# Layer 0 of a two-layer trunk: token halves joined at levels 32 and 64, and two recurrence chains stepped in one tick

## The chip, the cores and the metric

The kernel runs on one core of a Trainium2 chip. The metric is device microseconds (us) of one execution, as the median of several runs. Before the change the median of 3 runs was 2139.13 us (2138.96 to 2139.31). TensorE is called PE below, its weight loads PEld, VectorE DVE, ScalarE ACT, GpSimd POOL and SyncE SP.

## The reference

A decoder trunk of two layers over 256 tokens with 2048 features, all in float32. Layer 0 is the recurrent one, and the change lies in its mixer:

```
proj = h @ w_in                                   # 2048 -> 6144 columns
x_lru, y_lru, q_h, f_h, v_h, g_h = split(proj)    # 1024 columns each
lru  = rg_lru(conv(x_lru)) * gelu(y_lru)          # 4 heads, gated linear recurrence
hg   = hgrn2(q_h, f_h, v_h, g_h)                  # 8 heads of 128
mix  = concat([lru, hg]) @ w_out

# hgrn2, per head (lb is a learned lower bound)
q = silu(q_raw);  f = lb + (1 - lb) * sigmoid(f_raw);  k = (1 - lb) * sigmoid(-f_raw)
o[t] = sum over s <= t of (q[t] * prod(f[s+1..t]) . k[s]) v[s]
o    = rms_norm(o) * g_norm * silu(g_raw)
```

The reference runs hgrn2 in chunks of 64 tokens; written out over all tokens it is the sum above. After the mixer follow a residual add, a squared-ReLU MLP, and layer 1 with dilated attention and another MLP. Those parts aren't touched.

## The kernel before

**Products.** Every float32 operand is split into a high and a low float32r part, and a product is three matmuls: high times high, high times low, low times high. A *unit* is a weight block of 1 MB. SP loads it into a `raw` tile (L148), ACT casts it to `hi` (L130), DVE subtracts to get `lo` (L131). There are three tiles each of `raw`, `hi` and `lo`, and a unit is fetched three ahead, so the cast of a new unit waits until PE has released the tile of the unit that just ended.

**The input projection of layer 0** runs in *steps* of 512 output columns, in the order `ORDER` (L1150): v0 x0 x1 G0 q0 f0 q1 f1 G1 v1 g0 y0 g1 y1. The letter names the group, the digit its half. A step (`tokens_group`, `tokens`) takes four units of 24 matmuls each, 12 for either token half, and ends with two evictions (L371) into a `tk` tile. G0 and G1 aren't projections: they are the recurrence gates (`lru_gates`), 48 matmuls of 256 columns in four blocks of 12 that go in turn to a `p` bank and a `pl` bank.

**Ticks.** The rest of the mixer is interleaved by hand with the projection. After every 12 projection matmuls comes a *tick*: two to a unit, eight to a step. The table `TICKS` (L1151) says which lanes advance at each tick; a lane is a list of generators, and one advance runs to the next `yield`. PE executes in exactly the order that is written (`mm` and `turn` chain every matmul to the one before); the order on the other engines is made by the scheduler from priorities, and is fixed once the program is built. The lanes:

- **a** and **b**: `hgrn`, one generator for each pair of heads; lane a has chains 0 and 2, lane b chains 1 and 3. A chain has 12 steps: q (transpose, sigmoid), f (transpose, sigmoids), the diagonal (four matmuls of 128 columns into bank `pd` or `pt`), eight levels c = 1, 2, 4, ... 128, and the output (matmuls with v into `pd` or `pt`, squares, copy).
- **c**: `lru_in` four times (three steps each: transposes into bank `po` and a first convolution, a second convolution, a split into `bufb` by L269 and L270), then `lru_gelu` and `lru_out`.
- **e**: `lru_scan`, with Tanh, Exp and square roots on ACT and the scan on DVE.
- **d**: `finish`, two steps for each pair of heads: first the norm and the gate, on DVE, with a sigmoid; then four transposes into `po` and the split into `bufb` by L272 (ACT) and L273 (DVE).

**A level** of `hgrn` joins blocks of c tokens to blocks of 2c. For every pair of neighbouring blocks it needs the scores between keys of the first and queries of the second block. Up to level 64 it computes, for each of two heads and each token half of 128, one fp32 matmul: stationary all 128 keys of the half, moving the 64 queries that stand in second blocks (`halves(..., True)`), into a bank of `pl` (two buffers, shared by both chains and by G0 and G1). The wanted blocks are picked from it: up to level 16 by a masked copy on DVE (L532), at 32 and 64 by copies on ACT (L538, L540). Then a multiplication on DVE (L547) brings queries and keys to the next level, in place, and the products of decays (L550) go to a small scratch. Level 128 has one matmul of 128 columns per head (L523) and a copy (L524). The chain's data lie in `xall`: a slot of 2048 columns for a chain holds the queries and keys (1024), the decays f (512, last read at level 1) and the scratch.

`po`, `pd` and `pt` are one PSUM bank each, so a new use waits until the engines have read the last one. The weights that are waited for, the evictions and the chains' work share ACT and DVE in one queue each.

## Time and profile before

| what | value |
|---|---|
| median of 3 runs | 2139.13 us |
| the profiled execution | 2137.32 us |
| its span, first to last instruction | 2135.5 us |
| mean granted clock of PE | 0.998 |
| ACT busy | 1308.2 us, 61% |
| DMA | 500.12 MB, mean 234 GB/s |

The profile is of one execution. Timeline rows have the start in us from the span's start, the length, engine, line, operation, tiles and shapes; in brackets the idle time of the engine before it, and what ended that. `xN` merges N records that follow each other. A line can be that of a helper: L223 is every matmul, L226 every transpose, so the tile names tell the parts apart. An fp32 matmul leaves two records, a float32r matmul one. The ends of matmuls are modelled and overlap the next start, so what PE needs for something is read from start to next start. In rows of windows, the columns are the stretch and its length, the busy time and the count of PE, PEld, DVE, ACT and POOL, then the granted clock, the share of the DMA engines and GB/s.

In this execution the steps q0 to y1 lie at about 79 to 332 us of the span; G0 begins at 73.4 and G1 at 182.5.

### The profile page before, as it was taken

The numbers are of one execution on the slowest core, as the hardware profiler recorded it, in microseconds if no ns is written. First come the engines' busy times: TensorE is split into PE (matmuls) and PEld (weight loads), VectorE is DVE, ScalarE is ACT, GpSimd is POOL, SyncE is SP. The second block draws the span as 40 slices with busy tenths as digits, with TensorE's granted clock in tenths as the row PEclk, the third lists the DMA queues.
The fourth block names the chain that finished last, engine by engine and source line by source line (L and its number), as shares of the span: only waits on it lengthen the run. The fifth ranks groups of instructions, "written<-read, shape, count | busy, mean of one in ns | idle before, by whom it ended". The sixth has DMA issues, their size and how long they took to land.

```text
span 2135.5 us, 24906 instructions
## 1 busy us (share of the span) xinstructions
PE 2119.7 (99%) x9854; PEld 1766.3 (83%) x9854; DVE 1780.0 (83%) x1687; ACT 1308.2 (61%) x1307; POOL 72.3 (3%) x89
## 2 busy tenths in 40 slices
PE   9999999999999999999999999999999999999998
PEld 7888878888888888888888888888888888888887
DVE  7665758988888888889998888798988987988897
ACT  7646546666466566557665666566755755755664
POOL 0000000000000000000000000000000000000000
PEclk9999999999999999999999999999999999999999
DMA  8444446678878787887788667667878778787885
GB/s 342 179 166 150 157 179 205 212 244 266 250 243 258 255 253 234 278 248 242 223 285 247 215 217 213 220 206 238 246 236 280 240 249 263 249 250 241 273 261 157
DMA packets 70164, 500.12 MB, mean 234 GB/s; under 512 B 7840, under 2 KB 8096, under 8 KB 10272
## 3 DMA queue, kind: packets, MB, share of 16 engines
q1 hardware_dynamic: 57888, 412.99, 51.0%
q0 software_dynamic: 11872, 84.94, 21.3%
q8 instruction: 77, 1.26, 0.2%
q10 hardware_dynamic: 288, 0.61, 0.1%
q14 instruction: 39, 0.32, 0.0%
HBM read 496.41 MB, written 2.10 MB: 233 GB/s over the span
## 4 chain that ended last, share of the span: by engine, by line
PE 99%; DVE 1%; ACT 0%; DMA 0%; issue 0%
PE p L223 62%; PE pd L223 15%; PE po L223 14%; PE pt L223 3%; PE pl L226 2%; PE pl L223 2%; DVE lo L131 0%; ACT hi L130 0%; PE po L226 0%; DMA both_in<-in_head 0%; DVE xc L604 0%; PE pd L226 0%; PE pt L226 0%; ACT xall L1137 0%; ACT z L302 0%
## 5 line engine op out<-in xcount | busy, mean ns | idle before, releaser
L130 ACT CAST hi<-raw 128x2048 fp32r<-128x2048 f32 (+1 forms) x364 | 659.3, 1817 | 536.0 <-PE p L223 334.8
L131 DVE TENSOR_TENSOR lo<-raw,hi 128x2048 fp32r<-128x2048 f32 (+1 forms) x364 | 788.9, 2171 | 219.8 <-ACT hi L130 218.6
L223 PE MATMUL p<-hi,bufa 128*128 128x512 f32 x2000 | 650.4, 394 | 1.0 <-ACT bufa L272 1.0
L223 PEld LDWEIGHTS p<-hi,bufa 128*128 128x128 f32 x2000 | 376.1, 188 | 78.2 <-ACT bufa L272 1.2
L223 PE MATMUL p<-hi,bufb 128*128 128x512 f32 x1264 | 404.9, 390 | 0.0
L223 PE MATMUL p<-lo,bufa 128*128 128x512 f32 x1000 | 389.8, 390 | 0.0
L131 DVE TENSOR_TENSOR lo<-s,hi 128x2048 fp32r<-128x2048 f32 x120 | 274.2, 2285 | 12.0 <-ACT hi L130 9.7
L223 PEld LDWEIGHTS p<-hi,bufb 128*128 128x128 f32 x1264 | 237.3, 188 | 49.0
L130 ACT CAST hi<-s 128x2048 fp32r<-128x2048 f32 x120 | 229.6, 1913 | 50.4 <-PE po L223 22.5
L223 PE MATMUL p<-lo,bufb 128*128 128x512 f32 x632 | 245.9, 389 | 0.0
L223 PEld LDWEIGHTS p<-lo,bufa 128*128 128x128 f32 x1000 | 188.3, 188 | 37.5 <-DVE lo L131 0.4
L223 PEld LDWEIGHTS p<-lo,bufb 128*128 128x128 f32 x632 | 118.7, 188 | 24.2
L223 PE MATMUL pd<-hi,bufa 128*128 128x512 f32 x352 | 116.6, 393 | 0.0
L223 PE MATMUL p<-hi,formx 128*128 128x512 f32 x352 | 116.3, 391 | 0.0
L131 DVE TENSOR_TENSOR lo<-t,hi 128x2048 fp32r<-128x2048 f32 x40 | 91.5, 2288 | 15.7 <-ACT hi L130 15.7
L223 PE MATMUL po<-hi,bufb 128*128 128x512 f32 (+1 forms) x320 | 102.3, 386 | 0.0
L223 PE MATMUL p<-hi,formh 128*128 128x512 f32 x288 | 94.5, 389 | 0.0
L159 DVE TENSOR_TENSOR s<-s,raw 128x2048 f32<-128x2048 f32 x40 | 91.3, 2282 | 1.4 <-DMA raw<-in_w_qkv 1.4
L159 DVE TENSOR_TENSOR s<-raw,t 128x2048 f32<-128x2048 f32 x40 | 91.4, 2284 | 0.2 <-DMA raw<-in_w_o 0.2
L223 PE MATMUL po<-hi,bufa 128*128 128x512 f32 x256 | 84.8, 392 | 0.0
L130 ACT CAST hi<-t 128x2048 fp32r<-128x2048 f32 x40 | 76.5, 1914 | 11.6 <-PE pd L223 5.9
L223 PE MATMUL pd<-hi,bufb 128*128 128x512 f32 x256 | 83.0, 389 | 0.0
(317 smaller groups left out, 2783.0 us busy)
## 6 DMA issues: line engine op xcount, KB each, us to landing
raw<-in_w SPq DMA_DIRECT2D x224, 1024.0 KB, 6.6
raw<-in_w_in SPq DMA_DIRECT2D x45, 1024.0 KB, 4.8
raw<-in_w_qkv SPq DMA_DIRECT2D x42, 1024.0 KB, 6.6
t<-in_w SPq DMA_DIRECT2D x32, 1024.0 KB, 6.6
t<-in_w POOLq DMA_DIRECT2D x32, 1024.0 KB, 8.7
s<-in_w POOLq DMA_DIRECT2D x32, 1024.0 KB, 8.9
raw<-in_w_out SPq DMA_DIRECT2D x15, 1024.0 KB, 4.8
raw<-in_w_o SPq DMA_DIRECT2D x15, 1024.0 KB, 4.8
```

What stands on the lines that cost most here:

```text
L130: casts[:] = [after(A.copy(h, w), [])]
L131: i = V.tensor_tensor(l, w, h.bitcast(F32), OP.subtract)
L159: return V.tensor_tensor(held[to], held[x], held[y], OP.add)
L223: chain[:] = [after(T.matmul(*args, **kw), chain)]
L226: chain[:] = [after(T.transpose(out_, in_, ident), chain)]
```

## The change

Three things are altered, all in layer 0.

- At levels 32 and 64 the keys of first blocks are copied by ACT from both token halves into one contiguous tile `kc` of 128 columns per head (in the room of f), at the end of the level before. One matmul per head then takes `kc` as stationary and the 128 queries of second blocks of both halves as moving operand: two matmuls of 128 columns instead of four of 64. The diagonal blocks of the result are copied to the scores one by one: four copies at level 32 and two at level 64, where there were two and one.
- Lanes a and b advance in the same tick, every second tick, instead of in turn.
- The other lanes are placed around that. In x1 and f0 a tick is left free before the fourth step of lane c. Lane d begins in y0 and has its first four steps done by the end of g1. In y1 the ticks of c and d are apart, and those of o0 (the first step of the output projection) are one later.

```
             plf = pl.rearrange("p h j c -> p h (j c)")
...
-            for h in range(2):
-                for j in range(2):
-                    js = slice(j * P, j * P + P)
-                    mm(pl[:, h, j], kq[:, h, js], halves(qp[:, h, js], c, True), start=True, stop=True)
+            if c >= 32:
+                for h in range(2):
+                    mm(plf[:, h], kc[:, h], halves(qp[:, h], c, True), start=True, stop=True)
+            else:
+                for h in range(2):
+                    for j in range(2):
+                        js = slice(j * P, j * P + P)
+                        mm(pl[:, h, j], kq[:, h, js], halves(qp[:, h, js], c, True), start=True, stop=True)
...
-            elif c == 32:
-                for n in range(2):
-                    ps_ = slice(64 * n, 64 * n + 32)
-                    A.copy(st[ps_, :, :2, 64 * n + 32:64 * n + 64], pl[ps_, :, :, 32 * n:32 * n + 32])
             else:
-                A.copy(st[:64, :, :2, 64:], pl[:64])
+                for n in range(P // c):
+                    j, at_ = divmod(2 * n * c, P)
+                    ns = slice(n * c, n * c + c)
+                    A.copy(st[at_:at_ + c, :, j, at_ + c:at_ + 2 * c], plf[ns, :, ns])
...
             c *= 2
+            if c in (32, 64):
+                at_ = slot + 1024 + 256 * (c == 64)
+                kc = xall[:, at_:at_ + 256].rearrange("p (h s) -> p h s", h=2)
+                A.copy(kc.rearrange("p h (n c) -> p h n c", c=c),
+                       kq.rearrange("p h (n two c) -> p h n two c", two=2, c=c)[:, :, :, 0])
...
 TICKS = {
-    "x1": "c c c c c c . .",
+    "x1": "c c c . c c c .",
     "q0": ". e . e . e . e",
-    "f0": "c c c c c ac b .",
-    "q1": "a b a b a b a b",
-    "f1": "a b a b a b a b",
-    "v1": "a be a be a be a be",
-    "g0": "a b a b a b a b",
-    "y0": "a b a b a b a b",
-    "g1": "a b a b a b d d",
-    "y1": "dc dc d d dc dc . .",
-    "o0": ". . c c . . . .",
+    "f0": "c c c . c c abc .",
+    "q1": ". ab . ab . ab . ab",
+    "f1": ". ab . ab . ab . ab",
+    "v1": "e ab e ab e ab e ab",
+    "g0": ". ab . ab . ab . ab",
+    "y0": ". ab . ab . ab d ab",
+    "g1": ". ab d ab d ab . d",
+    "y1": "d c d d c d c c",
+    "o0": ". . . c c . . .",
 }
```

In the changed program the lines behind the edit stand eight lower (three to eight within `hgrn`): the score copies are L543, the level's multiplication is L550, the copy to `kc` is L559. L130, L131, L223, L226, L269 to L273 and L371 keep their numbers.

More of the change, by code (lines that the diff above doesn't have):

```diff
@@ L519, in hgrn @@
             pl = psc.tile([P, 2, 2, 64], F32, name="pl", bufs=2)
+            plf = pl.rearrange("p h j c -> p h (j c)")
             if c == 128:
-                plf = pl.rearrange("p h j c -> p h (j c)")
                 for h in range(2):
```

## Prediction

> **What bounds the kernel now.** I read the page first. Part 1 gives each engine's busy share, part 4 the chain of work that ended last.

> ```profile
> PE 2119.7 (99%) x9854; PEld 1766.3 (83%) x9854; DVE 1780.0 (83%) x1687; ACT 1308.2 (61%) x1307; POOL 72.3 (3%) x89
> PE 99%; DVE 1%; ACT 0%; DMA 0%; issue 0%
> ```

> TensorE (PE) is the bound over the whole span. A change gains only what it takes off PE's own instructions or off PE's waits, and any new PE wait is paid in full. The waits of PE come next: who waited for whom, total, times, longest.

> ```profile
> PE po L226 <- DVE bufb L273: 4.8, 1, 4.8
> ...
> PE po L226 <- DVE xc L604: 0.8, 2, 0.4
> ```

> One wait of 4.8 us and two of 0.4 lie in the changed stretch (53 to 345 us). The timeline around the long one, with the granted clock from windows (third quantity from the end):

> ```profile
> 301.27 0.60 PE L226 MATMUL po<-tab__183,ho 128*128 128x128 f32 x4
> ...
> 302.17 0.63 PE L223 MATMUL p<-hi,bufa 128*128 128x512 f32 x2
> ...
> 306.26 0.62 PE L223 MATMUL p<-hi,bufa 128*128 128x512 f32 x2
> ...
> 306.94 0.39 PE L223 MATMUL p<-hi,bufa 128*128 128x512 f32 x1
> 312.13 1.09 PE L226 MATMUL po<-tab__183,ho 128*128 128x128 f32 x4 [4.80 <-DVE bufb L273]
> ...
> 319.39 0.60 PE L226 MATMUL po<-tab__183,ho 128*128 128x128 f32 x4
> ```

> ```profile
> 307.37 1.90 ACT L130 CAST hi<-raw 128x2048 fp32r<-128x2048 f32 x1 [1.91 <-PE p L223]
> ...
> 309.30 2.29 DVE L131 TENSOR_TENSOR lo<-raw,hi 128x2048 fp32r<-128x2048 f32 x1 [0.30 <-ACT hi L130]
> 311.51 0.48 DVE L273 SCALAR_TENSOR_TENSOR bufb<-po,c__91,bufb 128x256 fp32r<-128x256 f32 x1
> ```

> ```profile
> 306.90:311.50 4.60, 0.43 (x2) 0.01 (x1) 4.30 (x8) 2.88 (x4) 0.00 (x0) 1.00 0.64 228
> 311.50:315.00 3.50, 2.87 (x9) 2.51 (x10) 2.89 (x10) 0.95 (x2) 0.00 (x0) 0.51 0.63 213
> ```

> Eighteen projection matmuls start between 302.17 and 306.26, so one costs 0.227 us. The next should have started at 307.17 but started at 312.13: 4.96 us lost. The reason is a queue. The weight cast (L130) waits until PE releases a weight tile at the end of a unit, its subtraction (L131) follows, and only then DVE frees the bank `po` (L273) that PE wants. Afterwards the clock is 0.51: from 312.13 to 319.39 are 7.26 us, against 307.17 - 301.27 = 5.90 for the same work before the wait. The slow clock cost another 1.36.

> **The change, part by part.** (a) *Two matmuls for four.* Levels 32 and 64 of four chains are 8 places. The four 64-column matmuls of a level are 8 records (fp32 leaves two each); the two 128-column ones would be 4, as level 128 has now.

> ```profile
> 178.02 1.00 PE L223 MATMUL pl<-xall 128*128 128x64 f32 x8
> 178.83 0.48 PE L223 MATMUL p<-hi,bufa 128*128 128x512 f32 x1
> ...
> 181.68 1.00 PE L223 MATMUL pl<-xall 128*128 128x64 f32 x8
> ```

> ```profile
> 198.39 0.60 PE L223 MATMUL pl<-xall 128*128 128x128 f32 x4
> 198.75 0.48 PE L223 MATMUL p<-hi,bufa 128*128 128x512 f32 x1
> ...
> 201.57 0.60 PE L223 MATMUL pl<-xall 128*128 128x128 f32 x4
> ```

> From start to next start: 0.81 and 0.36. A record costs about 0.11 whether 64 or 128 columns stream. Gain 8 x 0.45 = 3.6 us. The moving side is strided and level 128's is contiguous; the 64-column ones were strided too and show no surcharge, so I take none.

> [...]

> (b) *Steps side by side.* In the order of the built program, PE leaves the projection and comes back 24 times less. After a 64-column step, twelve projection matmuls take 181.68 - 178.83 = 2.85, after a 128-column step 201.57 - 198.75 = 2.82, against 12 x 0.227 = 2.73; with the records at 0.111 each, a return costs between 0.01 (0.36 + 2.82 - 2.73 - 4 x 0.111) and 0.04 (0.81 + 2.85 - 2.73 - 8 x 0.111). I take 0.03: gain 0.7, bounds 0.2 and 1.0.

> (c) *One tick more before the fourth `lru_in` step* in x1 and f0. The two waits of 0.4 end 2.7 us before the transposes now come. A modelled end lies 0.39 - 0.227 = 0.16 behind the next possible start, so each is worth 0.57: gain 1.1.

> (d) *Norms.* All four steps of group 0 come before y1, but the wait only moves. In the built order, `finish(1,0)`'s transposes want `po`, whose last reader is again an L273 behind an L130 and an L131 that wait for the end of a unit of y1: the same chain, with y1's tick 3 instead of tick 2, so twelve more projection matmuls (2.73) cover it. Left: 4.96 - 2.73 = 2.2. Gain 2.7.

> (e) *Clock.* A wait of 2.2 is under half of the one that dropped it. The nearest row on the other side is at the start, with a granted clock of 1.00 on both sides of it:

> ```profile
> 5.88 0.50 PE L223 MATMUL p<-hi,bufa 128*128 128x512 f32 x1 [0.97 <-ACT bufa L272]
> ```

> 0.97 kept the clock, 4.80 lost it. I take no drop (gain 1.4) and keep 1.4 per wait of over 2 us as the other end.

> (f) *New wait at G0.* The third `lru_in` step of x0's second half moves from tick 6 of x1 to tick 7. In the built order its split (L269, L270) now stands behind the last eviction of x1 (L371), one more cast and one more subtraction. Rows of before there:

> ```profile
> 70.08 2.29 DVE L131 TENSOR_TENSOR lo<-raw,hi 128x2048 fp32r<-128x2048 f32 x1 [0.80 <-ACT hi L130]
> ...
> 72.29 0.69 DVE L270 TENSOR_TENSOR bufb<-xc,bufb 128x512 fp32r<-128x512 f32 x1
> 73.38 0.40 PE L223 MATMUL p<-bufb,hi 128*128 128x256 f32 x2
> ...
> 74.81 0.40 PE L223 MATMUL pl<-bufb,hi 128*128 128x256 f32 x2
> ```

> ```profile
> 73.58 0.69 ACT L371 ACTIVATE tk<-p,nr 128x512 f32<-128x512 f32 x1 [2.03 <-PE p L223]
> 74.16 1.89 ACT L130 CAST hi<-raw 128x2048 fp32r<-128x2048 f32 x1
> ```

> With G0's start as zero (73.38): eviction at 0.20, cast at 0.78, done 2.67; subtraction 2.70; L270 starts 72.29 - 70.08 = 2.21 later, 4.91, done 5.60. PE needs it for G0's third block, two blocks of 74.81 - 73.38 = 1.43 in, second matmul: 2.98. Wait 2.6. Before, the split was done by 72.98, hidden.

> (g) *New wait at G1.* Both level-32 steps now sit at the end of f1 and fill both `pl` banks; G1's second block needs the first bank. ACT's order: eviction, cast, then eight copies (L543).

> ```profile
> 181.88 0.69 ACT L371 ACTIVATE tk<-p,nr 128x512 f32<-128x512 f32 x1 [2.30 <-PE p L223]
> 182.46 1.89 ACT L130 CAST hi<-raw 128x2048 fp32r<-128x2048 f32 x1
> ...
> 184.25 0.52 ACT L538 COPY st<-pl 32x128 f32<-32x128 f32 x2
> ```

> The copies begin 184.25 - 181.68 = 2.57 after the step's start. One of half the size is not in the trace: at most L538's 0.26, at least half of it; I take 0.21, four are done at 3.4. PE wants the bank at 2 x 0.45 + 1.43 = 2.3. Wait 1.1, bounds 0.8 and 1.4.

> (h) *New wait at level 128.* Its `pl` banks are freed by level 64's four copies, which ACT's order puts behind 2 casts, 2 sigmoids, 8 Tanh and Exp, 2 table loads and 3 square roots.

> ```profile
> 190.26 0.83 ACT L254 ACTIVATE bufb<-pl,c__91 128x256 f32<-128x256 f32 x2
> 190.98 1.30 ACT L254 ACTIVATE bufb<-bufb,sp 128x256 f32<-128x256 f32 x3
> 192.30 1.28 ACT L254 ACT_TABLE_LOAD   x1
> ...
> 197.42 0.72 ACT L254 ACTIVATE bufb<-bufb 128x256 f32<-128x256 f32 x2
> ```

> From v1's start: 0.2 + 2 x 1.8 + 0.7 + 8 x 0.42 + 2 x 1.3 + 3 x 0.34 = 11.5, the first two copies to 12.0, the next two (behind a square root) to 12.9. PE wants the banks after 48 x 0.227 + 0.9 = 11.8 and 0.45 later: waits of 0.2 and 0.4; I take 0.7 in all, bounds 0 and 1.4.

> (i) *Hidden.* The eight copies to `kc` and the smaller score copies add about 4 us to ACT over 150 us in which it is some 60% busy. A `kc` copy stands between DVE's multiplication and the matmul; if its cover went, it would cost PE 0.3 each, 2.4 in all. The eviction queued behind it feeds nobody for a tick. On SP, the two reloads now stand together before one last weight load; it was requested three units (over 16 us) ahead and lands in 4.8, so a late one is hidden too. From about 450 us on the order is the same.

> Sum: -3.6 - 0.7 - 1.1 - 2.7 - 1.4 + 2.6 + 1.1 + 0.7 = **-5.1**. The profiled execution took 2137.3 (span 2135.5 and 1.8 around it) and would take 2132.2; the median of 2139.1 lies 1.8 higher, so I predict 2134.0. The bounds of b, g and h together give 2132.7 to 2135.5.

> **Rivals.** *R1: the clock drops at G0 or at the norms.* For it: waits of 2.6 and 2.2 lie between 0.97 and 4.80. Against: they are nearer 0.97, and in the row of 4.80 the clock fell only 4.4 us after PE stopped (311.5 against 307.2). One drop gives 2135.4, two 2136.8. [...] *R2: columns, not records, set the cost* of (a); the rows of 0.81 and 0.36 speak against it. 2134.0 + 3.6 = 2137.6. *R3: the new ticks remove waits and add none* (no f, g, h, nothing left of d): 2134.0 - 2.6 - 1.1 - 0.7 - 2.2 = 2127.4. The orders of ACT and DVE speak against it. *R4, slower: DVE becomes the bound of the level steps.* Both chains' copies and products now follow one matmul pair, behind the unit's subtraction.

> ```profile
> 155.24 2.29 DVE L131 TENSOR_TENSOR lo<-raw,hi 128x2048 fp32r<-128x2048 f32 x1 [0.40 <-ACT hi L130]
> 157.45 0.42 DVE L532 COPY_PREDICATED st<-msk,pl 128x256 f32<-128x256 int8 x1
> 157.78 0.69 DVE L547 TENSOR_TENSOR xall<-xall 128x512 f32<-128x512 f32 x1
> ```

> Cast (2.1 with its release), 2.2, and twice 0.33 + 0.6 end 6.2 us after the unit; the next pair is due at 24 x 0.227 + 1.8 = 7.2. It decides from 1.0 us of lateness on: over some 20 steps, 1.5 us late loses 10 and gives 2144. Nothing in the rows makes it that late.

> **How the numbers follow.** Forecast 0.72; R1 0.13; R2 0.03; R3 0.05; R4 0.04; 0.03 for small waits not seen. I predict **2134.0**. From 2132.4 to 2136.6 lies the forecast with its bounds and R1 but for two full drops: 8 in 10. A measurement of this kernel can tell about 0.2% (4.3 us, so below 2134.9) from no change. Four fifths of the forecast and all of R3 lie below: faster 0.63; R1, R2 and the rest lie within: same 0.33; slower 0.04.

> **What would show it.** Level 32 and 64 steps as four records in 0.36; 16 matmuls less on PE. PE's waits: about 2.6 at G0 on L270, 1.1 in G1 on an ACT copy, two small ones before level 128, 2.2 on L273 near 311; none in x1 and f0. A granted clock of 1.00 throughout 60 to 345. Wrong if the clock falls, if a step waits for `kc`, or if a wait appears behind 345.

## The result and the profile after

| kernel | median, us | lowest and highest | runs |
|---|---|---|---|
| before | 2138.95 | 2137.50 to 2139.51 | 20 |
| after | 2134.99 | 2133.62 to 2135.88 | 20 |

The ratio is 0.9982 with a 95% interval of 0.9975 to 0.9989: 4.0 us less, or 0.18%. It lies 1.0 above the forecast of 2134.0 and inside its range, and it falls short of the 0.2% that the prediction called tellable by a tenth of a microsecond. The profiled execution took 2135.88 with a span of 2134.1.

The first line of the page and its chain of the work that ended last are nearly as before: PE still binds everything, and it has 32 records less, which are the 16 matmuls of the forecast.

```profile
PE 2118.3 (99%) x9822; PEld 1764.8 (83%) x9822; DVE 1778.8 (83%) x1687; ACT 1309.6 (61%) x1325; POOL 72.3 (3%) x89
PE 98%; ACT 1%; DVE 0%; DMA 0%; issue 0%; SPq 0%
```

The waits of PE, complete (who waited for whom: total, times, longest):

```profile
PE po L226 <- DVE bufb L273: 2.1, 1, 2.1
PE p L223 <- DVE bufb L270: 2.0, 1, 2.0
PE pl L223 <- ACT st L543: 1.1, 2, 1.0
PE po L283 <- DVE e L411: 1.1, 1, 1.1
PE p L223 <- ACT bufa L272: 1.0, 1, 1.0
PE p L223 <- ACT bufb L269: 0.2, 1, 0.2
```

The fourth and the fifth belong to the opening of the kernel, which is the same code as before. The wait of 4.8 has become 2.1, the two of 0.4 are gone, and new are 2.0 + 0.2 at G0 and 1.1 in all at G1 and level 128. In PE's timeline of after, first the joint step of two chains with G1 behind it, then G0, then the norms:

```profile
183.99 1.05 PE L223 MATMUL pl<-xall 128*128 128x128 f32 x8
184.80 0.49 PE L223 MATMUL p<-bufb,hi 128*128 128x256 f32 x2
...
187.46 0.50 PE L223 MATMUL pl<-bufb,hi 128*128 128x256 f32 x2 [0.98 <-ACT st L543]
```

```profile
73.28 0.40 PE L223 MATMUL p<-bufb,hi 128*128 128x256 f32 x2
...
76.52 0.38 PE L223 MATMUL p<-bufb,hi 128*128 128x256 f32 x1 [0.22 <-ACT bufb L269]
78.94 0.39 PE L223 MATMUL p<-bufb,hi 128*128 128x256 f32 x1 [2.03 <-DVE bufb L270]
```

```profile
311.16 0.39 PE L223 MATMUL p<-hi,bufa 128*128 128x512 f32 x1
313.64 0.63 PE L226 MATMUL po<-tab__183,ho 128*128 128x128 f32 x4 [2.10 <-DVE bufb L273]
```

Eight records, now a level of *two* chains, take 0.81 from start to next start; before, that was one chain. Behind both long waits stands what the forecast had left out. The windows of after (the granted clock is the third quantity from the end):

```profile
76.10:79.50 3.40, 1.15 (x7) 0.75 (x7) 3.24 (x4) 3.22 (x6) 0.00 (x0) 1.00 0.26 63
79.50:82.90 3.40, 3.40 (x18) 3.40 (x17) 0.73 (x2) 0.84 (x2) 0.00 (x0) 0.50 0.75 292
...
311.60:315.00 3.40, 1.36 (x8) 1.25 (x9) 3.40 (x8) 0.63 (x2) 0.00 (x0) 1.00 0.30 70
315.00:318.40 3.40, 3.40 (x9) 2.63 (x8) 1.09 (x3) 0.47 (x1) 0.00 (x0) 0.51 0.63 265
```

In each pair, a stretch with more than half of PE's time idle is followed by one at half clock. In the trace the slow stretches begin at 79.53 and 315.05 and last 3.41 us.

**Where the time went.** All times of this section are differences of start times in one trace. The changed part is cut at the first matmul of each stage: the first `lru_in` transposes (tick 1 of x1), G0, q0, G1, v1, and the first transpose for the MLP. Behind that cut, before and after differ by 0.03 us (1766.76 and 1766.74 to the start of PE's last matmul). Ahead of the changed part, in code that is the same in all kernels, the opening (from the first weight product, at about 5.9, to the first cut) lasts between 46.75 and 48.53 in the ten profiled executions, so single executions differ by up to 1.8 us without a reason in the change, and the table leaves the opening out. "(h)" marks a half-clock stretch.

| kernel | x1 to G0 | G0 | q0 to G1 | G1 | v1 to MLP | sum | against before |
|---|---|---|---|---|---|---|---|
| before | 20.60 | 5.75 | 103.36 | 5.84 | 172.01 (h) | 307.56 | |
| after | 19.99 | 10.01 (h) | 101.52 | 7.07 | 167.08 (h) | 305.67 | -1.9 |
| after, profiled again | 19.99 | 8.51 | 101.52 | 7.08 | 167.03 (h) | 304.13 | -3.4 |
| new matmuls, old ticks | 20.61 | 5.75 | 102.49 | 5.84 | 169.50 (h) | 304.19 | -3.4 |
| old matmuls, new ticks | 19.99 | 8.51 | 102.41 | 5.86 | 167.47 | 304.24 | -3.3 |
| after, PE kept busy | 19.99 | 8.51 | 101.52 | 7.08 | 165.52 | 302.62 | -4.9 |
| after, G0 mended | 19.99 | 5.75 | 101.52 | 7.08 | 167.10 (h) | 301.44 | -6.1 |
| after, norms mended | 19.99 | 9.97 (h) | 101.52 | 7.08 | 163.20 | 301.76 | -5.8 |
| after, both mended | 19.99 | 5.75 | 101.52 | 7.08 | 163.22 | 297.56 | -10.0 |
| all waits mended | 19.99 | 5.75 | 101.52 | 5.84 | 162.58 | 295.68 | -11.9 |

### The profile page after: what moved, and what is told of

It reads as the page before. It is cut to its first block, busy times and chain, and to the rows that moved or that the text cites. A ratio compares the mean times of both kernels' runs of the same rounds, so it can differ in the third digit from the quotient of the medians.

```text
span 2134.1 us, 24851 instructions
## 1 busy us (share of the span) xinstructions
PE 2118.3 (99%) x9822; PEld 1764.8 (83%) x9822; DVE 1778.8 (83%) x1687; ACT 1309.6 (61%) x1325; POOL 72.3 (3%) x89
## 4 chain that ended last, share of the span: by engine, by line
PE 98%; ACT 1%; DVE 0%; DMA 0%; issue 0%; SPq 0%
PE p L223 61%; PE pd L223 15%; PE po L223 14%; PE pt L223 3%; PE pl L226 2%; PE pl L223 2%; ACT hi L130 1%; DMA both_in<-in_head 0%; DVE lo L131 0%; ACT bufb L254 0%; PE po L226 0%; ACT bufa L272 0%; PE pd L226 0%; PE pt L226 0%; ACT L254 0%
## 5 line engine op out<-in xcount | busy, mean ns | idle before, releaser
L130 ACT CAST hi<-raw 128x2048 fp32r<-128x2048 f32 (+1 forms) x364 | 659.2, 1817 | 540.9 <-PE p L223 331.6
L131 DVE TENSOR_TENSOR lo<-raw,hi 128x2048 fp32r<-128x2048 f32 (+1 forms) x364 | 789.3, 2172 | 222.7 <-ACT hi L130 221.4
L223 PE MATMUL p<-hi,bufa 128*128 128x512 f32 x2000 | 644.3, 393 | 1.0 <-ACT bufa L272 1.0
L223 PEld LDWEIGHTS p<-hi,bufa 128*128 128x128 f32 x2000 | 376.3, 188 | 78.6 <-ACT bufa L272 1.2
L223 PE MATMUL p<-hi,bufb 128*128 128x512 f32 x1264 | 405.0, 391 | 0.0
L223 PE MATMUL p<-lo,bufa 128*128 128x512 f32 x1000 | 390.2, 390 | 0.1
L131 DVE TENSOR_TENSOR lo<-s,hi 128x2048 fp32r<-128x2048 f32 x120 | 274.3, 2286 | 11.2 <-ACT hi L130 8.8
L223 PEld LDWEIGHTS p<-hi,bufb 128*128 128x128 f32 x1264 | 237.3, 188 | 48.8
L130 ACT CAST hi<-s 128x2048 fp32r<-128x2048 f32 x120 | 229.6, 1913 | 51.5 <-PE po L223 22.3
L223 PE MATMUL p<-lo,bufb 128*128 128x512 f32 x632 | 245.9, 389 | 0.0
L223 PEld LDWEIGHTS p<-lo,bufa 128*128 128x128 f32 x1000 | 188.3, 188 | 38.7 <-DVE lo L131 0.9
L223 PEld LDWEIGHTS p<-lo,bufb 128*128 128x128 f32 x632 | 118.7, 188 | 24.3
L223 PE MATMUL pd<-hi,bufa 128*128 128x512 f32 x352 | 116.6, 393 | 0.0
L223 PE MATMUL p<-hi,formx 128*128 128x512 f32 x352 | 116.3, 391 | 0.0
L131 DVE TENSOR_TENSOR lo<-t,hi 128x2048 fp32r<-128x2048 f32 x40 | 91.5, 2288 | 15.7 <-ACT hi L130 15.7
L223 PE MATMUL po<-hi,bufb 128*128 128x512 f32 (+1 forms) x320 | 102.3, 386 | 0.0
L223 PE MATMUL p<-hi,formh 128*128 128x512 f32 x288 | 94.5, 389 | 0.0
L223 PE MATMUL po<-hi,bufa 128*128 128x512 f32 x256 | 84.8, 392 | 0.0
L130 ACT CAST hi<-t 128x2048 fp32r<-128x2048 f32 x40 | 76.5, 1914 | 11.6 <-PE pd L223 5.9
L223 PE MATMUL pd<-hi,bufb 128*128 128x512 f32 x256 | 83.0, 389 | 0.0
```

Of the source, the lines that this page charges most:

```text
L130: casts[:] = [after(A.copy(h, w), [])]
L131: i = V.tensor_tensor(l, w, h.bitcast(F32), OP.subtract)
L223: chain[:] = [after(T.matmul(*args, **kw), chain)]
```

## The experiments

The theory at the start (A in the expectations): the sum of the prediction holds, and what is missing is the clock, which drops behind a wait of about 2 us in some executions and not in others (R1, per execution). The rivals (B): some term of the sum is too good (matmuls or ticks bring less than counted), or the waits of 2 us are cheap to PE in some way and the loss is elsewhere.

**The change again, and its two halves.** The kernel after was run anew beside one with the new matmuls under the old `TICKS`, and one with the old matmuls under the new `TICKS`. There is no diff beyond the two parts of the change.

> The changed kernel again, on the chip of the three kernels beside it. Theory A (the terms of the sum hold; what is missing went to the clock, which drops in or behind the two waits of over 2 us, by where the wait falls in a window of 3.4 us): about 4.0 us below before, single runs spread over some 2 us, and in the trace up to two stretches of 3.4 us at half clock. Theory B (the clock costs no more than before; the missing us are that a level's two matmuls save less than the trace of before promised, or that leaving the projection less often saves nothing): the same 4.0 us, with less spread.

> The joined matmuls alone, with the table of ticks of before. The waits should be those of before (4.8 us at the norms, two of 0.4), none at G0, G1 or level 128. A: 3.6 to 4.2 us below before, since 16 fp32 matmuls at 0.22 go and nothing else changes. B: 1.8 us or less below before.

> The new table of ticks alone, with four matmuls of 64 columns at levels 32 and 64 and no copies to kc. Waits of 2.6 us at G0 and 2.2 at the norms, none at G1 or at level 128. A: it gives back the 3.6 of the matmuls but not the waits of 1.1 and 0.6 at G1 and level 128, so 1.5 to 2.5 us below before. B: 3.5 us or more below before.

| kernel | median (lowest to highest), us | before, same chip | ratio, 95% interval |
|---|---|---|---|
| after again | 2135.13 (2133.51 to 2135.77) | 2137.99 | 0.9984 [0.9975, 0.9993] |
| new matmuls, old ticks | 2134.81 (2133.74 to 2136.11) | 2137.99 | 0.9984 [0.9975, 0.9993] |
| old matmuls, new ticks | 2134.09 (2133.79 to 2138.48) | 2137.99 | 0.9986 [0.9977, 0.9995] |

Each half alone brings what the whole brings. By the table of stretches they should have added up: -3.4 and -3.3 give -6.7, and only the score copies that the new matmuls bring (their waits are in G1 and at level 128, 1.23 + 0.56) belong to both together; -4.9 is what is left of the sum. By the medians two expectations were missed: the new matmuls brought 3.2 where A had 3.6 to 4.2, and the new ticks 3.9 where A had 1.5 to 2.5 and B at least 3.5. A's figure for the ticks starts from the 4.0 of after, drops included (4.0 - 3.6 + 1.1 + 0.6 = 2.1), and the trace of that run, below, has no drop; its median alone would speak for B. The second execution of after shows one half-clock stretch where the first had two, with 8.51 against 10.01 in G0: one drop there costs 1.50 us. With old ticks PE's waits are those of before (4.8, and twice 0.4), and the level's joint matmuls do what was counted. Waits and timeline of the new matmuls under old ticks:

```profile
PE po L226 <- DVE bufb L273: 4.8, 1, 4.8
```

```profile
181.89 0.61 PE L223 MATMUL pl<-xall 128*128 128x128 f32 x4
182.25 0.49 PE L223 MATMUL p<-bufb,hi 128*128 128x256 f32 x2
```

A step of one chain takes 0.36 instead of 0.81, as before's rows said. The two steps of level 32 in the stretch q0 to G1 gain 103.36 - 102.49 = 0.87, the six others 172.01 - 169.50 = 2.51: 3.4 of the 3.6. With new ticks and old matmuls the waits are those of after at G0 and the norms, and none at G1 or level 128:

```profile
PE po L226 <- DVE bufb L273: 2.1, 1, 2.1
PE p L223 <- DVE bufb L270: 2.0, 1, 2.0
```

Its trace has these two waits and no half-clock stretch between 60 and 345 us. Seven of its eleven times lie between 2133.79 and 2134.15 and four up to 4.7 higher; the mean granted clock of the run is 0.999 in eight and 0.997 in the three slowest. The same waits do or do not drop the clock, by execution.

**PE kept busy in the two waits.** To take the drops away and leave the waits, PE gets useless fp32 matmuls of the identity, into banks that nobody reads at that point, where it would stand still: ten ahead of G0's third block, nine ahead of the first transposes of `finish(1, 0)`.

```diff
+    def keep_warm(name, n):
+        p = psc.tile([P, 2, 2, P], F32, name=name, bufs=1)
+        for _ in range(n):
+            mm(p[:, 0, 0], ident, ident, start=True, stop=True)
...
+        if g and not half:
+            keep_warm("pt", 9)
...
+            if (gp, m) == (0, 2):
+                keep_warm("pd", 10)
```

> The changed kernel with useless fp32 matmuls (10 and 9, about 2 us each time, into a bank that nobody reads) put where PE waits at G0 and at the norms: the waits stay as long, but PE is busy in them. A: no stretch at half clock between 60 and 350 us, and 1 to 3 us less than the changed kernel. B: the same time as the changed kernel within 0.5 us.

The median is 2132.47 (2132.16 to 2133.90) against 2137.99 of before: 0.9974 [0.9964, 0.9984], and 2.7 us less than after in the same comparison, for more work. In its timeline the twenty records fill what was idle, and G0's third block starts no earlier for it; in its windows the clock is full over the whole stretch:

```profile
75.72 2.39 PE L223 MATMUL pd<-tab__183 128*128 128x128 f32 x20
...
78.50 0.39 PE L223 MATMUL p<-bufb,hi 128*128 128x256 f32 x1 [0.28 <-DVE bufb L270]
```

```profile
60.00:345.00 285.00, 283.45 (x1492) 242.01 (x1491) 190.33 (x283) 162.65 (x248) 0.00 (x0) 1.00 0.48 169
```

The stretches sum to -4.9, where the prediction without a drop had -5.1. The rival that the sum itself was wrong falls; its single terms are compared below. Against this kernel the first execution of after lost 1.50 at G0 and 167.08 - 165.52 = 1.56 at the norms, both to the clock.

**The waits removed.** They come from the order of ACT and DVE, so the order is changed, not the wait. At G0 the weight cast that stands ahead of x0's last split is made to follow that split (`first_` hands the split's copy to the next cast as one it has to come after). At the norms the tick of the second `finish` step of y1 moves behind the split that it waits for.

```diff
-            casts[:] = [after(A.copy(h, w), [])]
+            casts[:] = [after(A.copy(h, w), first_)]
+            del first_[:]
...
-        split_to(bufb[:, b0:b0 + 2], xc[:, b0:b0 + 2])
+        i = split_to(bufb[:, b0:b0 + 2], xc[:, b0:b0 + 2])
+        if (n, half) == (0, 1):
+            first_.append(after(i, []))
```

```diff
-    "y1": "d c d d c d c c",
+    "y1": "d c c d d c d c",
```

The first diff alone, the second alone, and both:

> The changed kernel with one order added: the cast that stood ahead of x0's last split waits for it, so the split is ready when G0 wants it. No wait at G0; the others stay. A (each wait over 2 us costs itself and, in part of the executions, 1.5 us of half clock): 2.7 to 4.2 us less than the changed kernel, at most one stretch at half clock (behind the norms), G0 in 5.8 us. B (the waits cost themselves alone): 2.7 less.

> The changed kernel with one tick more between the two steps of finish(1,0): y1 becomes d c c d d c d c. No wait at the norms; G0's stays. A: 2.2 to 3.7 us less than the changed kernel, at most one stretch at half clock (in G0). B: 2.2 less.

> Both of these: no wait over 1.3 us is left in layer 0. A: no stretch at half clock between 60 and 350 us in any execution, so the single runs lie closer together (the start of the kernel still varies by about 1 us), and 5 to 8 us less than the changed kernel. B: 4.9 less, with the same spread.

| kernel | median (lowest to highest), us | before, same chip | ratio, 95% interval |
|---|---|---|---|
| G0 mended | 2131.67 (2129.42 to 2132.80) | 2137.88 | 0.9968 [0.9955, 0.9980] |
| norms mended | 2131.51 (2130.29 to 2132.25) | 2137.88 | 0.9969 [0.9957, 0.9981] |
| both mended | 2127.60 (2127.21 to 2128.61) | 2137.88 | 0.9952 [0.9939, 0.9965] |

The waits of the three, in this order: with G0 mended the one at the norms is left, with the norms mended the one at G0, with both neither, and the longest is 1.0.

```profile
PE po L227 <- DVE bufb L275: 2.1, 1, 2.1
...
PE pl L224 <- ACT st L545: 1.2, 2, 1.0
```

```profile
PE p L223 <- DVE bufb L270: 2.0, 1, 2.0
...
PE pl L223 <- ACT st L543: 1.2, 2, 1.0
```

```profile
PE pl L224 <- ACT st L545: 1.2, 2, 1.0
```

Kept busy, PE lost the waits alone; with both mended it loses neither waits nor clock. The difference between these two kernels is the price of the waits: 302.62 - 297.56 = 5.1 by the stretches (2.76 at G0, 2.30 at the norms), 2132.47 - 2127.60 = 4.9 by the medians. After, with the waits and the drops behind them, stands 2135.13 - 2127.60 = 7.5 above "both mended". (These medians come from two comparisons, in which before lay at 2137.99 and 2137.88.)

**All waits removed.** On top of both, the cast at G1 is made to follow the score copies of level 32 of the first two chains, and their copies of level 64 go from ACT to DVE, in whose queue the trace of after has no table load (it has 11, of 1.28 us each, all on ACT).

```diff
-                    A.copy(st[at_:at_ + c, :, j, at_ + c:at_ + 2 * c], plf[ns, :, ns])
+                    copy = V.tensor_copy if c == 64 and g == 0 else A.copy
+                    i = copy(st[at_:at_ + c, :, j, at_ + c:at_ + 2 * c], plf[ns, :, ns])
+                    if c == 32 and g == 0:
+                        first_.append(after(i, []))
```

> Both of these, and the waits at G1 and level 128 taken away: the cast ahead of the level-32 copies waits for them, and level 64's score copies of chains 0 and 1 go to DVE. No wait of PE above 0.3 us from 53 to 345 us. A and B alike: 1.7 us less than with both alone; 11 to 12 us less than before the change, about what rival R3 gave (11.7 less than before).

The median is 2125.70 (2125.63 to 2127.19) against 2137.88: 0.9944 [0.9931, 0.9957], 12.2 us less than before and 1.9 less than with both mended. PE's waits are those of the opening alone, and from 60 to 345 us it is busy throughout:

```profile
PE po L285 <- DVE e L413: 1.1, 1, 1.1
PE p L224 <- ACT bufa L274: 0.8, 1, 0.8
```

```profile
60.00:345.00 285.00, 285.00 (x1484) 243.30 (x1483) 197.58 (x298) 164.32 (x249) 0.00 (x0) 1.00 0.50 176
```

This is the fastest kernel of the study. R3 of the prediction, new ticks without new waits, was worked out at 11.7 less; it is about what the change would have brought with ACT's and DVE's order mended.

**From which wait on the clock drops.** In the MLP of layer 0, where PE has no waits of its own, 32 waits of graded length are put into the last kernel, once for each of two probes: a transpose of a small tile, a chain of POOL memsets on that tile, a transpose again. The first probe has chains of 1 to 8 memsets, the second of 5 to 12 (`n + 5` in the diff), about 0.26 us a step. Both add work that nobody reads, and their times (2192.11 and 2240.30, one run each) say nothing else.

```diff
+    def gap():
+        n = gaps[0] % 8
+        gaps[0] += 1
+        p = psc.tile([P, 2, P], F32, name="pt", bufs=1)
+        turn(p[:, 0], gz)
+        with urgent():
+            for _ in range(n + 1):
+                nc.gpsimd.memset(gz, 1.0)
+        turn(p[:, 1], gz)
...
+        probes = {2: gap, 6: gap} if (src is w1 or src is w2) and i0 < 64 else {}
...
+            if len(did) in probes:
+                probes[len(did)]()
```

> A measure of the clock by itself: the version without waits, and in the MLP of layer 0 32 waits of PE of graded length, each on a chain of 1 to 8 GpSimd memsets (about 0.5 to 2.8 us if one takes 0.3) between two useless transposes. A: no stretch at half clock behind the waits under 1.2 us, one of 3.4 us behind part of those over 2 us, at a rate that grows with the length, and all stretches begin at times that differ by a multiple of 3.41 us, so that the place of a wait in such a window decides. B: none, or as many behind short waits as behind long ones.

> The same with 5 to 12 memsets in a chain (about 1.8 to 4.2 us). A: a stretch at half clock behind nearly every wait over 3 us. B: no rise with the length.

The length of a wait doesn't decide by itself. In the first probe a wait of 1.96 dropped the clock and one of 2.22 did not (timeline, the rows around each):

```profile
568.73 0.27 PE L227 MATMUL pt<-tab__183,gz 128*128 128x128 f32 x1
571.22 0.33 PE L227 MATMUL pt<-tab__183,gz 128*128 128x128 f32 x1 [2.22 <-POOL gz L783]
```

```profile
731.46 0.27 PE L227 MATMUL pt<-tab__183,gz 128*128 128x128 f32 x1
733.68 0.33 PE L227 MATMUL pt<-tab__183,gz 128*128 128x128 f32 x1 [1.96 <-POOL gz L783]
```

```profile
731.22:734.63 3.41, 1.46 (x7) 0.81 (x6) 3.41 (x4) 3.27 (x2) 1.43 (x7) 1.00 0.00 0
734.63:738.04 3.41, 3.41 (x10) 2.62 (x9) 3.41 (x4) 0.44 (x1) 0.11 (x1) 0.50 0.83 286
567.38:570.79 3.41, 1.62 (x8) 1.06 (x6) 1.76 (x3) 1.86 (x1) 1.32 (x7) 1.00 1.00 420
570.79:574.20 3.41, 2.98 (x14) 2.48 (x15) 2.29 (x1) 0.03 (x1) 0.32 (x2) 1.00 0.88 344
```

The 1.96 lies in one window, which has 1.95 idle (3.41 - 1.46), and the next window runs at half clock. The 2.22 is cut in 1.79 and 0.43, and no window drops; the one behind them has a clock of 1.00 too. The second probe has longer ones: a wait of 2.74 cut in 1.87 and 0.88 kept the clock, a wait of 3.01 with 2.02 in one window lost it. Its rows:

```profile
758.35 0.33 PE L227 MATMUL pt<-tab__183,gz 128*128 128x128 f32 x1 [3.01 <-POOL gz L783]
```

```profile
927.88 0.33 PE L227 MATMUL pt<-tab__183,gz 128*128 128x128 f32 x1 [2.74 <-POOL gz L783]
```

```profile
756.33:759.75 3.42, 1.40 (x7) 1.18 (x8) 3.42 (x4) 2.22 (x2) 1.56 (x8) 1.00 0.28 65
759.75:763.16 3.41, 3.41 (x10) 2.64 (x9) 3.41 (x2) 0.00 (x0) 0.86 (x1) 0.50 0.78 264
```

In all windows at full clock of both probes up to 1.87 us of idle time kept the clock, and from 1.95 on lost it for the next window. There is one longer stretch: in the second probe a wait of 3.27 left 2.14 idle in the window before 974.79 and 1.13 in the half-clock window behind it, and the window from 978.21 to 981.62 was at half clock too. Why 1.13 was enough there is not shown; these runs have this one case.

By these windows, a wait of 2.1 us drops the clock if at least some 1.9 of it (1.87 kept it, 1.95 lost it) fall into one window. That is so for (3.41 - 2.1 + 2 x 0.2) / 3.41 = 0.5 of the positions that it can have on the grid, an estimate that takes all positions as equally likely. One of 4.8 has at least 2.4 in one window in any position; in before, the window of 308.17 to 311.58 lies wholly in it, and the clock is 0.50 in the next, to 314.99. The count over both probes fits: the clock dropped behind none of 32 waits of up to 1.70, behind 10 of 20 of 1.95 to 2.48, 1 of 4 of 2.74 and 7 of 8 of 3.01 and 3.27.

The waits of the changed kernel fit these figures. In its first profiled execution the half-clock stretches begin 315.05 - 79.53 = 235.52 apart, 69 periods of 3.413, and the windows ahead of them have 2.25 and 2.04 idle. In its second profiled execution the wait at G0 is divided by the grid and leaves 1.59 in one window, with no drop (the next window has a clock of 1.00), and the wait at the norms leaves 2.10 and drops the clock:

```profile
78.16:81.58 3.42, 1.83 (x15) 1.83 (x16) 2.30 (x4) 2.21 (x6) 0.00 (x0) 1.00 0.28 101
...
310.32:313.73 3.41, 1.31 (x9) 0.88 (x8) 3.41 (x6) 0.86 (x4) 0.00 (x0) 1.00 0.41 127
313.73:317.14 3.41, 3.41 (x10) 2.67 (x9) 1.70 (x6) 0.86 (x2) 0.00 (x0) 0.50 0.73 291
```

The mean granted clock of each run, on record to three digits, tells how often it happens without a profile. One drop takes about 3.41 x 0.5 / 2134 = 0.0008 off it. It is 0.999 in all 18 runs of the three kernels in which PE stands still for no more than 1.0 us in the changed part (PE kept busy, both mended, all waits mended). With one of the two waits left it is 0.999 in six of twelve runs and 0.998 in six, which is the half. In after it is 0.998 in all 31 runs, so hardly any of them can have gone without a drop: one or two in each, 1.5 or 3.1 us. Why most runs of the old matmuls under the new ticks went without one and those of after did not is not shown.

## Why the prediction was right, and where it was not

The sum was right as a total, and the time came out above the forecast for one step: **(e)**. That it came out only 1.0 above is in part luck. R1, which is what happened, stands at 2135.4 and 2136.8 in the prediction; the stretches of the two profiled executions give 1.9 and 3.4 less than before, where the forecast had 5.1, and run again, after lay 2.9 below before and not 4.0. The opening, which differs between executions by more than a drop costs, is in all the medians.

- **(a) Two matmuls for four**: 3.6 forecast, 0.87 + 2.51 = 3.4 measured with the new matmuls alone. Between 64 and 128 columns the records of these fp32 matmuls set the cost, not the columns (0.81 for eight records of 64, 0.36 for four of 128, 0.81 for eight of 128), and R2 falls. Between 256 and 512 columns the cost does follow the columns in these traces: the 48 float32r matmuls of 256 in G0 take 5.75, 0.12 each, and those of 512 take 0.227.
- **(b) Steps side by side**: 0.7 forecast. New ticks alone gain 103.36 - 102.41 = 0.95 in q0 to G1, of which the wait of (c) in f0 should be 0.57: 0.38 for nine returns. From v1 on they gain 4.54, of which 2.7 and 1.4 are the norms' wait and clock: 0.4. Together 0.8.
- **(c) A tick more before the fourth step**: 0.57 in each place forecast, 20.60 - 19.99 = 0.61 measured in x1; in f0 it was not measured by itself.
- **(d) Norms**: a wait of 2.2 forecast, 2.10 measured and 0.16 of a modelled end beside it. The reason, the L273 behind an L130 and an L131, is that of the waits' row.
- **(f) G0**: 2.6 forecast; 0.22 + 2.03 of idle time, and a stage longer by 8.51 - 5.75 = 2.76. The queue is as read from the built order. In the timelines of ACT and DVE of after the eviction, the cast, the subtraction and both halves of the split follow each other as the prediction wrote them:

```profile
73.48 0.69 ACT L371 ACTIVATE tk<-p,nr 128x512 f32<-128x512 f32 x1 [2.03 <-PE p L223]
74.06 1.90 ACT L130 CAST hi<-raw 128x2048 fp32r<-128x2048 f32 x1
75.85 0.62 ACT L269 CAST bufb<-xc 128x512 fp32r<-128x512 f32 x1
```

```profile
75.99 2.29 DVE L131 TENSOR_TENSOR lo<-raw,hi 128x2048 fp32r<-128x2048 f32 x1 [2.29 <-ACT hi L130]
78.20 0.68 DVE L270 TENSOR_TENSOR bufb<-xc,bufb 128x512 fp32r<-128x512 f32 x1
```

- **(g) G1**: 1.1 forecast; 0.98 of idle time, the stage 7.08 - 5.84 = 1.24 longer.
- **(h) Level 128**: 0.7 forecast. From v1 to the MLP the halves give -2.51 and -4.54, the whole without drops 165.52 - 172.01 = -6.49: 0.56 for this wait. Only 0.16 of it shows as idle time of PE, at 204.6; the rest must lie under modelled ends. With the wait removed the stretch gains 163.22 - 162.58 = 0.64.
- **(i) Hidden**: PE's waits have no row for `kc`, nor for DVE in the level steps, so R4 didn't come. ACT is busy 1.4 us longer with 18 instructions more, where the prediction had about 4.
- **(e) "I take no drop"** is the step that failed. The clock dropped behind both waits in the first profiled execution and behind one in the second, so R1 came, to which the prediction gave 0.13, and a fall of the clock stands in its own list of what would be wrong. The step put a wait of 2.2 between two rows, 0.97 that kept the clock and 4.80 that lost it, and took the nearer. But what counted in the probes is not the nearer row. It is how much idle time fell into one window (1.87 kept the clock, 1.95 lost it), and for a wait of 2.1 about half of the positions suffice, by the estimate above. The second reason, that the clock fell only 4.4 us after PE stopped, read a delay out of one row: the probe's window of 731.22 to 734.63 has PE stopped at 731.73 and back at 733.68, and the clock fell at its end, 2.9 after PE stopped. The price of 1.4 a drop was right (1.50 and 1.56).

Of the 2.7 us between after and the kernel with PE kept busy, one drop would explain 1.5 and both together 3.1; 2.7 lies between. How many of the unprofiled runs had both is not told by a clock of three digits, and a part may also lie in the opening; this stays open.

## What to carry to other kernels

PE was busy for 99% of the span here, and a saved instruction counted nearly in full (3.4 of the 3.6) and a new wait too (0.22 + 2.03 of idle time at G0 made the stage 2.76 longer): this change saved 12 us of work and stalls and gave two thirds back in waits, and clock drops behind them, that came from the order of two other engines' queues, where one large weight cast stood ahead of a small piece that PE needed. So after moving a step, read the built order of the engines that feed it, and let the large, early work follow the small, urgent one. By these runs, count a wait of the matrix engine of two to three microseconds as that wait and, in about half of the cases (behind 11 of the 24 waits of 1.95 to 2.74 in the probes), a clock drop of 1.5 us on top. Several short waits should be better than one long one, by an estimate from the 32 waits of up to 1.70, none of which dropped the clock. This was not tried, nor was how near to each other they may lie.

## What the runs showed of the hardware

**The opening has half pace too, and in one execution its end fits the grid.** The opening of after, in its second profiled execution, is slow until about 9.9 us, where the kernel with PE kept busy is at full pace from about 7. Three matmuls take 7.65 - 6.37 = 1.28 in the one and 7.87 - 7.18 = 0.69 in the other:

```profile
6.37 0.63 PE L223 MATMUL p<-lo,bufa 128*128 128x512 f32 x1
...
7.65 0.63 PE L223 MATMUL p<-lo,bufa 128*128 128x512 f32 x1
```

```profile
7.18 0.39 PE L223 MATMUL p<-lo,bufa 128*128 128x512 f32 x1
...
7.87 0.39 PE L223 MATMUL p<-lo,bufa 128*128 128x512 f32 x1
```

The code is the same, the granted clock of 5 to 10 us reads 1.00 in both, and the half pace is seen only in the pitch. Its end at about 9.9 (three matmuls take 1.28 up to 8.93, and 0.69 from 10.10 on) and the half-clock stretch of that execution at 313.73 lie 89 windows of 3.413 apart. The openings of the profiled executions differ by up to 1.8 us, and a good part of it seems to be this: between these two it is 48.32 - 46.96 = 1.4 us, before the change is even reached. The three longest openings of the ten, 48.3 to 48.5, are the three in which the half pace ends late (at about 9.9, 10.4 and 10.6); the other seven lie between 46.8 and 47.7.
